# Merge projections of two branches: pairs of tiles by seven block products in place of eight

## The chip, the cores and the metric

The kernel runs on one core of a Trainium2 chip. The metric is the time of one execution on the device in microseconds (us). In the profile the engines are PE (TensorE, matrix products; PEld is its loading of weights), DVE (VectorE), ACT (ScalarE), POOL (GpSimd) and SP (SyncE, which issues most DMAs). Plain loads and stores are issued from SP; DMAs that add to what their destination holds (accumulating DMAs) are issued from POOL.

## What is computed

One layer of a hybrid backbone for 128 context tokens and 512 latent tokens, 640 in all, of width 1024. A gated long convolution (branch h) and an attention (branch a) each give 1024 channels per token. The step that the change touches is the merge of the two:

```python
def merge_branches(y_h, g_h, y_a, g_a, m, w_bh, w_ba, w_out):
    p_h = (y_h * jax.nn.silu(g_h)) @ w_bh
    p_a = (y_a * jax.nn.silu(g_a)) @ w_ba
    m_h, m_a = jnp.split(jax.nn.sigmoid(m), 2, axis=-1)
    return (m_h * p_h + m_a * p_a) @ w_out
```

A residual and a layer norm follow. Everything is float32. The gates m come from the layer's input h by one large projection, which also gives queries, keys, values and the convolution's inputs.

## The kernel before, in words

Activations lie transposed: channels on the 128 partitions, the 640 tokens along the row. A projection tile gives 128 output channels: 8 blocks of 128 input channels (k), for each three passes, and for each pass two matmuls over 320 tokens each, so 48 matmuls of 128x128 weights by 128x320 data. The three passes replace one float32 product: `split` (L96 to L99) writes a high part on ACT (float32r) and the remainder on DVE, and `accumulate` (L160 to L169) adds high x high, low x high and high x low in PSUM. `wtile` (L130 to L148) loads the weights of a tile (512 KB) into the buffer raw (two of them) and splits them into wh (two) and wl (three). With `eng="dma"` the remainder is made otherwise: ACT writes the negative of the raw weights, rounded to float32r, into wl (L142), an accumulating DMA from POOL adds the weights from DRAM to that, which leaves the remainder (L143), and ACT writes wh (L144).

In order of time the kernel does: a prologue; four quarters of the convolution branch, whose results stay in SBUF as eight tiles yh; the attention by pairs of heads, whose results stay as eight tiles ya; woven with it the gate tiles `mix_h` (tanh of half the gate's projection). Then comes the part that is changed. Two tiles of `mix_a` are computed, yh is split, and for n from 0 to 7 the projection T_BH + n is computed from yh and multiplied by (1 + tanh) on DVE (L993), while ya is split. Then, for each n, the next `mix_a` tile, the projection T_BA + n from ya, its gating (L1023), the sum of both branches (L1024) and the split of the sum. `gate_rows` (eight rows of the modulation weights, 16 small matmuls for each two) and `gate_bias` run beside this. Last, five output tiles (L1065) with their norms (L1081 to L1104).

The code is recorded with a tile framework. Its scheduler sets the order of each engine's instructions, by its own forecast of durations, when the kernel is built; on the chip each engine then runs its list strictly in that order, and so do the DMA queues of SP and POOL. During prologue and attention PE's order is that of the code. A buffer of a pool is written again only when its last reader is done, and a DMA that waits for that holds up those behind it on its queue.

Of the kernel before, what the change touches and what calls it, by code (L numbers as in the profile page):

```python
# [15 lines left out]
D = 1024  # L16
LP = 128
LS = 512
NK = 8
# [26 lines left out]
def tile_hyena_natten_step(ctx: ExitStack, tc: tile.TileContext, a, o):  # L46
# [57 lines left out]

    out = {"yh": {}}

    def load_pack(i):
# [10 lines left out]

    hH = hp.tile([P, NK, NT], F32R, tag="hH", name="hH")
    hL = hp.tile([P, NK, NT], F32R, tag="hL", name="hL")  # L120
    st = const.tile([P, NK, 32], F32, tag="st", name="st")
# [48 lines left out]

    def proj(i, xh=None, xl=None, eng=None):
        if i in banks:
            return banks.pop(i)
        w = wtile(i, eng)
        ps = bank(i)
        for k in range(NK):
            accumulate(ps, w, k, xh[k] if xh else hH[:, k], xl[k] if xl else hL[:, k])
            if k < NK - 1:
                yield
        return ps  # L180
# [60 lines left out]
    def prologue():  # L241
# [7 lines left out]
        def work(items, ps):  # L249
            for item in items.split():  # L250
                if item[0] == "w":
                    for _ in range(int(item[1:])):
                        nc.tensor.matmul(ps[:, 256:], hid[:, :P], hid[:, :256], start=True, stop=True, skip_group_check=True)  # L253
                else:
                    i, j = int(item[0]), int(item[1])
                    accumulate(banks[i], early[i], j, hH[:, j], hL[:, j], lead=(0, 1, 2) if j < 1 else (0, 2, 1))

# [18 lines left out]
        for k in range(NK):  # L276
# [32 lines left out]
            for c, s0, n in ((0, PC, LP), (1, SC, LS)):  # L309
                cs = slice(s0, s0 + n)  # L310
                nc.vector.tensor_scalar(hx[:, cs], xt[:, cs], mod[:, 1, c : c + 1], mod[:, 0, c : c + 1], op0=ALU.mult, op1=ALU.add)
                nc.scalar.activation(hH[:, k, cs], xt[:, cs], AF.Identity, scale=mod[:, 1, c : c + 1], bias=mod[:, 0, c : c + 1])  # L312
            nc.vector.tensor_tensor(hL[:, k], hx[:], f(hH[:, k]), op=ALU.subtract)  # L313
            if k == 0:
# [336 lines left out]
    yh, ident = out["yh"], out["ident"]  # L651

# [53 lines left out]
    def values(m):  # L706
# [5 lines left out]
        def passes(k):  # L712
            wh, wl = w[k // 4][0][k % 4], w[k // 4][1][k % 4]
            return ((hH, wh, k == 0, False), (hL, wh, False, False), (hH, wl, False, k == NK - 1))

        for half in range(2):
            ks = range(4 * half, 4 * half + 4)
            for k in ks:
                for x, wk, first, last in passes(k):
                    for t in range(4):  # L720
                        nc.tensor.matmul(  # L721
                            ps[:, t // 2, t % 2 * 256 : t % 2 * 256 + 256], x[:, k, P * t : P * t + P], wk,
                            start=first and t % 2 == 0, stop=last, skip_group_check=True,
                        )
                yield
            if half:
                nc.scalar.activation(v[:, :1024], ps[:].rearrange("p a b -> p (a b)"), AF.Copy)
            else:
                pe = ps_mm.tile([P, 2, 512], F32, tag="mm", name=f"ve{m}")[:, 0]
            for k in ks:  # L730
                for x, wk, first, last in passes(k):
                    nc.tensor.matmul(pe[:, :256], x[:, k, P * 4 :], wk, start=first, stop=last, skip_group_check=True)  # L732
            yield
# [14 lines left out]

    tail = ctx.enter_context(ExitStack())
    ac = ctx.enter_context(ExitStack())  # L750
    ya, tms, edges, biases = [], [], {}, {}

    def attention_setup():
        nonlocal at, mask
        hy.close()
        yap = out["yap"] = tail.enter_context(tc.tile_pool(name="yap", bufs=1, side="right"))
        ya.extend(row(yap, "ya", f"ya{j}", bufs=NK) for j in range(NK))
        at = ac.enter_context(tc.tile_pool(name="at", bufs=1, side="right"))
# [107 lines left out]

    def gated(j, cols, o_):
        nc.vector.tensor_tensor(ya[j][:, cols], out[f"sg{j}"][:, cols], o_, op=ALU.mult)

# [17 lines left out]
    def tiled(i):  # L887
# [39 lines left out]
    def gate_a(j):  # L927
        out[f"sg{j}"] = sg = at.tile([P, NT], F32, tag="sg", bufs=2, name=f"sg{j}") if j else row(yhp, "yh", "sg0")
        yield from gate_tile(T_GA + j, sg[:])
        yield  # L930

    def mix_h():
        homes = ((0, "q"), (0, "k"), (0, "v"), (), (0, "ql"), (0, "kl"), (1, "q"), (1, "ql"))
        for n in range(NK):
            th = slot(*homes[n], f"mh{n}") if homes[n] else th
            th, pair = (pair[:, NT:], None) if n == 3 else (th[:, :NT], th)
# [24 lines left out]

    mp = tail.enter_context(tc.tile_pool(name="mp", bufs=1, side="right"))
    lp = left.enter_context(tc.tile_pool(name="lp", bufs=1))
    gpart = slot(1, "v", "gpart")[:, :D]
    yhH = [row(lp, "yhH", f"yhH{n}", F32R, NK) for n in range(NK)]
    yhL = []
    yaH = [row(mp, "yaH", f"yaH{n}", F32R, NK) for n in range(NK)]
    yaL = []

# [9 lines left out]
    def mix_a(n):  # L979
        ps = now(proj(T_MA + n))[2]  # L980
        th = mp.tile([P, NT], F32, tag="th", bufs=3, name=f"mta{n}")
        nc.scalar.activation(two(th[:]), ps[:, :, :HALF], AF.Tanh, scale=0.5)
        return th

    side = gate_rows()
    mtas = [mix_a(0), mix_a(1)]
    for n in range(NK):
        yhL.append(row(yhp, "yh", f"yhL{n}", F32R))
        split(yhH[n][:], yhL[n][:], yh[n][:])
    for n in range(NK):  # L990
        th = out[f"mh{n}"]
        ps = now(proj(T_BH + n, yhH, yhL))[2]
        nc.vector.scalar_tensor_tensor(two(th), two(th), 1.0, ps[:, :, :HALF], op0=ALU.add, op1=ALU.mult)  # L993
        yaL.append(row(out["yap"], "ya", f"yaL{n}", F32R, NK)[:] if n else slot(1, "kl", "yaL0", F32R)[:, :NT])
        split(yaH[n][:], yaL[n], ya[n][:])
        next(side, None)
    mH, mL = yhH, yhL
    gbc = lp.tile([P, 2, D], F32, tag="gbc", name="gbc")
    eps = lp.tile([P, 1], F32, tag="eps", name="eps")
    nc.gpsimd.memset(eps[:], LN_EPS)  # L1000

    def gate_bias():
        selr = lp.tile([P, 2], F32R, tag="selr", name="selr")
# [3 lines left out]
        gt = out["slots_r"].tile([P, 2, 384], F32R, tag="k", name="gt")  # L1007
        for c0, n in ((0, 384), (384, 384), (768, 256)):
# [8 lines left out]

    for n in range(NK):
# [4 lines left out]
        nc.vector.scalar_tensor_tensor(two(th[:]), two(th[:]), 1.0, ps[:, :, :HALF], op0=ALU.add, op1=ALU.mult)  # L1023
        nc.vector.tensor_tensor(th[:], th[:], out[f"mh{n}"], op=ALU.add)  # L1024
        split(mH[n][:], mL[n][:], th[:])
        next(side, None)
        if n == 4:
            gate_bias()

    wo = []  # L1030
    woh = lp.tile([P, D], F32R, tag="woh", name="woh")
    wol = wp.tile([P, D], F32R, tag="wl", bufs=3, name="wol0")
    wohH = hp.tile([P, 5, D], F32R, tag="hH", name="wohH")
    wolH = hp.tile([P, 5, D], F32R, tag="hL", name="wolH")
    for k in range(NK):
        raw = wp.tile([P, D], F32, tag="raw", name=f"wo{k}")
        load_to(raw[:], a["wall"][T_WO + k])
        if k == 0:
            wo.append((woh[:], wol[:]))
        elif k < 6:  # L1040
            wo.append((wohH[:, k - 1], wolH[:, k - 1]))
        else:
            wh = wp.tile([P, D], F32R, tag="wh", name=f"woh{k}")
            wl = wp.tile([P, D], F32R, tag="wl", bufs=3, name=f"wol{k}")
            wo.append((wh[:], wl[:]))
        split(*wo[k], raw[:])


    tail.close()
    fin = ctx.enter_context(tc.tile_pool(name="fin", bufs=1, side="right"))  # L1050
    bc = fin.tile([P, 2, D], F32, tag="bc", name="bc")
    def out_tile(t, split_cols):
# [188 lines left out]
```

## Time and profile before

| | us |
|---|---|
| median of 3 runs | 927.14 (926.0 to 927.77) |
| the profiled execution | 925.7 |
| its span in the profile | 923.9 |

The mean granted clock of TensorE in the span is 0.997 of full speed. Lines such as `L166 PE MATMUL mm<-hH,wh 128*128 128x320 f32 x1120 | 263.3, 313 | 0.9` are groups: line of the kernel, engine, operation, output tile and input tiles, shape, count, then busy time in us and mean ns of one, then the idle time of the engine just before them in us. A row of a table by stage has the stretch in us, its length, the busy time of PE, PEld, DVE, ACT and POOL with the counts, the granted clock, the share of the 16 DMA engines that was busy, and GB/s. A row of the waits names who waited for whom, the total in us, how often, and the longest. A row of the DMA issues ends with the median us from issue to landing; a row of the DMA queues has packets, MB and the share of the 16 engines' span. Rows of the timeline begin with start and length in us.

### The profile page before, as it was taken

The numbers are of one execution on the slowest core, as the hardware profiler recorded it, in microseconds if no ns is written. First come the engines' busy times: TensorE is split into PE (matmuls) and PEld (weight loads), VectorE is DVE, ScalarE is ACT, GpSimd is POOL, SyncE is SP. The second block draws the span as 40 slices with busy tenths as digits, with TensorE's granted clock in tenths as the row PEclk, the third lists the DMA queues.
The fourth block names the chain that finished last, engine by engine and source line by source line (L and its number), as shares of the span: only waits on it lengthen the run. The fifth ranks groups of instructions, "written<-read, shape, count | busy, mean of one in ns | idle before, by whom it ended". The sixth has DMA issues, their size and how long they took to land.

```text
span 923.9 us, 16758 instructions
## 1 busy us (share of the span) xinstructions
PE 910.2 (99%) x6856; PEld 877.4 (95%) x6856; DVE 486.4 (53%) x948; ACT 380.4 (41%) x776; POOL 146.2 (16%) x188
## 2 busy tenths in 40 slices
PE   8999999999999999999999999999999999999996
PEld 7899999999999999999999999999999999999885
DVE  4776775693796676445352533432261223335676
ACT  4485455554545334255454544444261112223200
POOL 0011010110010000474454543331000000000000
PEclk9999999999999999999999999999999999999998
DMA  8966664655465113242222221212123343224631
GB/s 320 380 161 135 128 149 98 137 133 123 100 141 126 50 49 85 86 122 67 71 68 69 67 70 58 72 49 70 48 69 113 120 146 99 72 69 116 205 114 69
DMA packets 36553, 102.13 MB, mean 111 GB/s; under 512 B 4316, under 2 KB 13020, under 8 KB 36477
## 3 DMA queue, kind: packets, MB, share of 16 engines
q1 hardware_dynamic: 32300, 86.35, 28.9%
q0 software_dynamic: 4032, 14.68, 9.8%
q8 instruction: 54, 0.88, 0.4%
q14 instruction: 23, 0.18, 0.1%
q10 hardware_dynamic: 144, 0.03, 0.0%
HBM read 97.38 MB, written 3.67 MB: 109 GB/s over the span
## 4 chain that ended last, share of the span: by engine, by line
PE 95%; DVE 2%; ACT 2%; issue 1%; POOL 0%; POOLq 0%
PE mm L166 65%; PE out L1065 6%; PE v L721 5%; PE s L788 2%; PE s L831 2%; PE pt L824 2%; PE ve L732 1%; PE adaT L236 1%; PE adaT L253 1%; PE yb L151 1%; PE yb L153 1%; PE yb L152 1%; PE gate L236 0%; PE fl L384 0%; PE fl L385 0%
## 5 line engine op out<-in xcount | busy, mean ns | idle before, releaser
L166 PE MATMUL mm<-hH,wh 128*128 128x320 f32 x1120 | 263.3, 313 | 0.9 <-ACT hH L312 0.6
L166 PE MATMUL mm<-hH,wl 128*128 128x320 f32 x1120 | 259.7, 310 | 0.4 <-DVE wl L99 0.4
L166 PE MATMUL mm<-hL,wh 128*128 128x320 f32 x1120 | 259.1, 310 | 0.0
L99 DVE TENSOR_TENSOR wl<-raw,wh 128x1024 fp32r<-128x1024 f32 x66 | 81.6, 1237 | 231.9 <-ACT wh L98 231.7
L166 PEld LDWEIGHTS mm<-hH,wh 128*128 128x128 f32 x1120 | 186.7, 188 | 6.2 <-issue 4.2
L166 PEld LDWEIGHTS mm<-hH,wl 128*128 128x128 f32 x1120 | 188.0, 188 | 1.4 <-DVE wl L99 1.1
L166 PEld LDWEIGHTS mm<-hL,wh 128*128 128x128 f32 x1120 | 188.2, 188 | 1.1 <-DVE hL L313 0.5
L98 ACT ACTIVATE wh<-raw 128x1024 fp32r<-128x1024 f32 x66 | 69.8, 1059 | 216.8 <-PE mm L166 95.9
L143 POOL DMA_DIRECT2D wl<-wall x28 | 24.3, 869 | 264.0 <-ACT wl L142 208.8
L144 ACT ACTIVATE wh<-raw 128x1024 fp32r<-128x1024 f32 x28 | 29.7, 1060 | 42.9 <-PE mm L166 42.7
L808 POOL TENSOR_SCALAR p<-p,sm 128x384 f32<-128x384 f32 x32 | 42.1, 1326 | 27.7 <-DVE sm L807 27.7
L1095 POOL TENSOR_TENSOR r<-r,bc 128x64 f32<-128x64 f32 x1 | 0.3, 320 | 249.7 <-ACT r L1094 249.7
L808 POOL TENSOR_SCALAR edge<-edge,sm 128x320 f32<-128x320 f32 x32 | 35.5, 1121 | 0.0
L474 DVE SCALAR_TENSOR_TENSOR x<-zs,pack,x 128x641 f32<-128x641 f32 x32 | 28.3, 884 | 12.1 <-ACT x L472 12.0
L826 ACT ACTIVATE pts<-pt 128x384 f32<-128x384 f32 x64 | 26.2, 502 | 11.0 <-PE pt L824 11.0
L142 ACT ACTIVATE wl<-raw 128x1024 fp32r<-128x1024 f32 x28 | 30.0, 1071 | 0.0
L166 PE MATMUL mm<-yhH,wh 128*128 128x320 f32 x128 | 29.9, 315 | 0.0
L166 PE MATMUL mm<-yaH,wh 128*128 128x320 f32 x128 | 29.2, 309 | 0.0
L166 PE MATMUL mm<-yhL,wh 128*128 128x320 f32 x128 | 29.2, 309 | 0.0
L166 PE MATMUL mm<-yaH,wl 128*128 128x320 f32 x128 | 29.2, 309 | 0.0
L166 PE MATMUL mm<-yaL,wh 128*128 128x320 f32 x128 | 29.2, 309 | 0.0
L166 PE MATMUL mm<-yhH,wl 128*128 128x320 f32 x128 | 29.2, 309 | 0.0
(330 smaller groups left out, 1677.7 us busy)
## 6 DMA issues: line engine op xcount, KB each, us to landing
raw<-wall SPq DMA_DIRECT2D x96, 512.0 KB, 3.6
wl<-wall POOLq DMA_DIRECT2D x28, 512.0 KB, 5.8
ada<-wada SPq DMA_DIRECT2D x16, 512.0 KB, 8.1
gate<-wada SPq DMA_DIRECT2D x8, 512.0 KB, 3.7
wo<-wall SPq DMA_DIRECT2D x8, 512.0 KB, 3.7
xt<-xT SPq DMA_DIRECT2D x8, 320.0 KB, 8.1
dec<-decay SPq DMA_DIRECT2D x20, 128.0 KB, 3.5
x<-xB SPq DMA_DIRECT2D x5, 512.0 KB, 3.8
```

The source lines that it names most:

```text
L98: hi = nc.scalar.activation(dst_h, src, AF.Copy)
L99: return hi, (eng or nc.vector).tensor_tensor(dst_l, src, f(dst_h), op=ALU.subtract)
L142: nc.scalar.activation(wl, raw[:], AF.Copy, scale=-1.0)
L143: nc.gpsimd.dma_start(wl, a["wall"][i], accum_op=ALU.add)
L144: nc.scalar.activation(wh, raw[:], AF.Copy)
L166: nc.tensor.matmul(ps[hf][:, :HALF], wt[k], x[:, hf * HALF : (hf + 1) * HALF], start=(i == 0 and k == 0), stop=(i == lead[2] and k == NK - ...
L474: nc.vector.scalar_tensor_tensor(d, zs[:, c : c + NG], convw[:, i, c : c + 1], d, op0=ALU.mult, op1=ALU.add)
L721: nc.tensor.matmul(ps[:, t // 2, t % 2 * 256 : t % 2 * 256 + 256], x[:, k, P * t : P * t + P], wk, start=first and t % 2 == 0, stop=last, ...
L788: nc.tensor.matmul(dst[h], x[rows(h), qs], y[rows(h), ks], start=i == 0, stop=i == 2, skip_group_check=True)
L808: nc.gpsimd.tensor_scalar_mul(pv, pv, sm[:, 2:3])
L826: nc.scalar.activation(ptS[:], pt[:, :384], AF.Copy)
L1065: ins = nc.tensor.matmul(dst, m[k][:, c0 : c0 + P], w[:, c : c + n], start=(first and k == 0), stop=(last and k == NK - 1), skip_group_che ...
```

## The change

The 16 projection tiles of the merge are computed in pairs. For a pair, the 256 output channels and 1024 input channels form a 2x2 block matrix (blocks of 512 input by 128 output channels), and the branch's rows a 2x2 block matrix too (512 channels by 320 tokens). Their product is formed with seven block products by Winograd's form of Strassen's method. Each product is 4 k-blocks x 3 passes = 12 matmuls of 128x320. Sums and differences of blocks come from these places:

- `token_blocks`: yh and ya are written to DRAM when they are ready (16 stores from SP), read back as blocks of 4 x 320 per partition, combined by three subtractions on DVE and one accumulating DMA, and each of the seven is split, once per branch.
- `weight_blocks`: for each pair seven half-tiles of 256 KB are loaded. Two are negated on ACT, four sums (s3, s2, s1, s4) are made by accumulating DMAs; five of the seven are split on ACT and DVE, two (a12, a22) by ACT and an accumulating DMA. Each raw tile has one buffer. The split parts take turns in the five buffers wh (two) and wl (three).
- `pair_product`: the seven products go into four PSUM banks named x, y, v and z, in the order x, y, v, z, x, v, z; between them steps on ACT and DVE form the four results and multiply by the gates.

All eight `mix_a` tiles now come first, ahead of the products. The hL and hH tiles are held as halves, and their memory is used again for token blocks and output weights. Output weights are split during the last pair; `gate_bias` comes after the products.

```diff
     def gate_conv(n):
         if n in half_done:
             gapped_product(out["yh"][n], out[f"u{n // 2}"][n % 2])
+            nc.sync.dma_start(yh_d[n], out["yh"][n][:])
...
             prompt_values(j, spare.pop(0))
+            nc.sync.dma_start(ya_d[j], ya[j][:])
...
+    def token_blocks(src, name):
+        def raw(i, j):
+            t = mg.tile([P, 4, HALF], F32, tag="braw", bufs=4, name=f"{name}{i}{j}")
+            load_to(t[:], src[4 * i : 4 * i + 4, :, HALF * j : HALF * j + HALF].rearrange("k p t -> p k t"))
+            return t[:].rearrange("p k t -> p (k t)")
...
+        t1, t3, t2, t4 = raw(0, 0), raw(0, 1), raw(1, 1), raw(1, 0)
+        yield done(t1, 0)
+        nc.vector.tensor_tensor(t1, t3, t1, op=ALU.subtract)
+        nc.vector.tensor_tensor(t3, t2, t3, op=ALU.subtract)
+        nc.vector.tensor_tensor(t2, t1, t2, op=ALU.subtract)
+        yield done(t2, 1)
+        yield done(t3, 2)
+        yield done(t1, 3)
+        yield done(t4, 4)
+        nc.gpsimd.dma_start(t4, t2, accum_op=ALU.add)
+        yield done(t4, 5)
+        yield done(raw(1, 1), 6)
...
+    def weight_blocks(i0, i1):
+        w0, w1 = ([a["wall"][i][:, 512 * h : 512 * h + 512] for h in range(2)] for i in (i0, i1))
...
+        def halves(r, src=None):
+            n, n_weights[0] = n_weights[0] % 5, n_weights[0] + 1
+            tag = ("wh", "wl", "wh", "wl", "wl")[n]
+            t = wp.tile([P, 2, 512], F32R, tag=tag, bufs=3 if tag == "wl" else 2, name=f"wb{i0}_{n}")
+            if src is None:
+                split(t[:, 0], t[:, 1], r)
+            else:
+                nc.scalar.activation(t[:, 1], r, AF.Copy, scale=-1.0)
+                add(t[:, 1], src)
+                nc.scalar.activation(t[:, 0], r, AF.Copy)
+            return t
+
+        a11 = raw("a11", w0[0])
+        s3, s2 = raw("s3", w1[0]), raw("s2", w1[1])
+        for t in (s3, s2):
+            nc.scalar.activation(t, t, AF.Copy, scale=-1.0)
+        add(s3, w0[0])
+        add(s2, s3)
+        yield halves(a11)
+        yield halves(s2)
+        yield halves(s3)
+        s1 = raw("s1", w1[0])
+        add(s1, w1[1])
+        yield halves(s1)
+        yield halves(raw("a12", w0[1]), w0[1])
+        yield halves(raw("a22", w1[1]), w1[1])
+        s4 = raw("s4", w0[1])
+        add(s4, s2)
+        yield halves(s4)
...
+        for n, t in enumerate("xyvzxvz"):
...
+            w = next(weights)
+            xh, xl = xb(n)
+            for k in range(4):
+                wh, wl = (w[:, i, P * k : P * k + P] for i in range(2))
+                for i, (wk, x) in enumerate(((wh, xh), (wh, xl), (wl, xh))):
+                    nc.tensor.matmul(
+                        dst[t], wk, x[:, k], start=n < 4 and k == 0 and i == 0, stop=k == 3 and i == 2, skip_group_check=True,
+                    )
+            next(step)
+            yield
...
+    for m in range(4):
+        for n, _ in enumerate(pair_product(T_BH + 2 * m, T_BH + 2 * m + 1, out[f"mh{2 * m}"], out[f"mh{2 * m + 1}"], from_yh)):
...
+    for m in range(4):
+        for n, _ in enumerate(pair_product(T_BA + 2 * m, T_BA + 2 * m + 1, mtas[2 * m], mtas[2 * m + 1], from_ya)):
...
-    for n in range(NK):
-        th = mtas.pop(0)
-        if n + 2 < NK:
-            mtas.append(mix_a(n + 2))
-        ps = now(proj(T_BA + n, yaH, yaL))[2]
```

Here `add(dst, src)` is an accumulating DMA from POOL, `raw` a load from SP, and `mg` the pool of the raw tiles.

In the order that the scheduler gives the changed program, PE takes the first product of a pair ahead of the last two of the pair before, and for most pairs then v, y, x (the fifth product), z. The pairs are numbered 0 to 7 below.

More of the change, by code (lines that the diff above doesn't have):

```diff
@@ L650, in tile_hyena_natten_step @@
               8 * NK, N_CONV + N_BACK + N_FILTER)
[L651 removed]
+    ident = out["ident"]
     def rows(h):
@@ L731, in values @@
                 for x, wk, first, last in passes(k):
-                    nc.tensor.matmul(pe[:, :256], x[:, k, P * 4 :], wk, start=first, stop=last, skip_group_check=True)
+                    nc.tensor.matmul(pe[:, :256], x[:, P * 4 :], wk, start=first, stop=last, skip_group_check=True)
             yield
@@ L980, in mix_a @@
         ps = now(proj(T_MA + n))[2]
-        th = mp.tile([P, NT], F32, tag="th", bufs=3, name=f"mta{n}")
+        th = row(yhp, "yh", f"mta{n}")
         nc.scalar.activation(two(th[:]), ps[:, :, :HALF], AF.Tanh, scale=0.5)
-        return th
-    side = gate_rows()
-    mtas = [mix_a(0), mix_a(1)]
-    for n in range(NK):
[L988 to L996, printed above, removed]
@@ L997, in tile_hyena_natten_step, with block, done @@
-    mH, mL = yhH, yhL
-    gbc = lp.tile([P, 2, D], F32, tag="gbc", name="gbc")
-    eps = lp.tile([P, 1], F32, tag="eps", name="eps")
+        return th[:]
+    n_blocks = [0]
+    def block(name):
+        n, n_blocks[0] = n_blocks[0] % 8, n_blocks[0] + 1
+        pool, tag = (blkp, "blk") if n < 4 else (hp, H_TAGS[n - 4])
+        return pool.tile([P, 2, 4 * HALF], F32R, tag=tag, name=name)
+    def token_blocks(src, name):
[3 more added lines that the diff above has]
+            return t[:].rearrange("p k t -> p (k t)")
+        def done(r, n):
+            b = block(f"{name}b{n}")
+            split(b[:, 0], b[:, 1], r)
+            return [b[:, i].rearrange("p (k t) -> p k t", k=4) for i in range(2)]
+        t1, t3, t2, t4 = raw(0, 0), raw(0, 1), raw(1, 1), raw(1, 0)
[10 more added lines that the diff above has]
+        yield done(raw(1, 1), 6)
@@ new lines, in tile_hyena_natten_step, with out_weight @@
+    mH, mL, wo = [], [], []
+    def out_weight(k):
+        raw = wp.tile([P, D], F32, tag="raw", name=f"wo{k}")
+        load_to(raw[:], a["wall"][T_WO + k])
+        t = block(f"wo{k}")
+        wo.append((t[:, 0, :D], t[:, 1, :D]))
+        split(*wo[k], raw[:])
+    for _ in side:
+        pass
+    for m in range(4):
+        for n, _ in enumerate(pair_product(T_BA + 2 * m, T_BA + 2 * m + 1, mtas[2 * m], mtas[2 * m + 1], from_ya)):
+            if m == 3:
+                if n == 0:
+                    out_weight(0)
+                out_weight(n + 1)
+        ns = (2 * m, 2 * m + 1)
+        for n in ns:
+            nc.vector.tensor_tensor(mtas[n], mtas[n], out[f"mh{n}"], op=ALU.add)
+        for n in ns:
+            mH.append(row(yhp, "yh", f"mH{n}", F32R)[:])
+            mL.append(merge_home(n, "mL", F32R))
+            split(mH[n], mL[n], mtas[n])
@@ L1016, in gate_bias @@
                 nc.vector.scalar_tensor_tensor(gbc[:, c, cs], b0[:, cs], 0.25, pg[:, :n], op0=ALU.mult, op1=ALU.add)
-    for n in range(NK):
-        th = mtas.pop(0)
-        if n + 2 < NK:
-            mtas.append(mix_a(n + 2))
-        ps = now(proj(T_BA + n, yaH, yaL))[2]
[L1023 to L1051, printed above, removed]
+    gate_bias()
     def out_tile(t, split_cols):
```

119 lines of the change are left out of this document (95 added, 24 removed).

## Prediction

> **What bounds the kernel now.** I read the page first: busy time, slices, DMA queues, chain of waits.
>
> ```profile
> span 923.9 us, 16758 instructions
> ...
> PE 910.2 (99%) x6856; PEld 877.4 (95%) x6856; DVE 486.4 (53%) x948; ACT 380.4 (41%) x776; POOL 146.2 (16%) x188
> ...
> PEclk9999999999999999999999999999999999999998
> DMA  8966664655465113242222221212123343224631
> GB/s 320 380 161 135 128 149 98 137 133 123 100 141 126 50 49 85 86 122 67 71 68 69 67 70 58 72 49 70 48 69 113 120 146 99 72 69 116 205 114 69
> ...
> q1 hardware_dynamic: 32300, 86.35, 28.9%
> q0 software_dynamic: 4032, 14.68, 9.8%
> ...
> PE 95%; DVE 2%; ACT 2%; issue 1%; POOL 0%; POOLq 0%
> ```
>
> PE is busy for 910.2 of 923.9 us and carries 95% of the chain: every other engine has slack and the DMA engines are one to four tenths busy in the second half. Then the waits of PE, and its busy time in the stretch that the change rebuilds.
>
> ```profile
> PE adaT L253 <- POOL spare L268: 1.5, 1, 1.5
> PE fp L152 <- DVE sl L99: 1.1, 1, 1.1
> ```
>
> ```profile
> 696.70:850.00 153.30, 153.30 (x1133) 150.17 (x1132) 50.80 (x57) 34.38 (x40) 0.00 (x0) 1.00 0.32 103
> ```
>
> The longest wait of PE in the whole run is 1.5 us, and from 696.7 to 850 us it does not idle at all (153.30 of 153.30). So a matmul taken out here shortens the run by its full time, and every wait put in lengthens it by its full time; there is no slack on PE to absorb one.
>
> **What is taken from PE.** The two branch projections are six groups of 128 matmuls (first and last by the groups by line), and the timeline gives their spacing.
>
> ```profile
> L166 PE MATMUL mm<-yhH,wh 128*128 128x320 f32 x128 | 29.9, 315 | 0.0
> ...
> L166 PE MATMUL mm<-yhH,wl 128*128 128x320 f32 x128 | 29.2, 309 | 0.0
> ```
>
> ```profile
> 696.72 0.46 PE L166 MATMUL mm<-yhH,wh 128*128 128x320 f32 x2
> ...
> 703.47 0.46 PE L166 MATMUL mm<-yhH,wl 128*128 128x320 f32 x2
> ```
>
> One tile is 24 such rows of two. From the first start to the last are 23 steps: 6.75 / 23 = 0.2935 us, or 0.1467 us per matmul (the 309 ns are its latency; they overlap). Before: 6 x 128 = 768, or 112.7 us. The changed program holds 8 pairs x 7 products x 12 = 672, or 98.6 us. **PE gains 14.1 us.** In the old order two neighbours share their weights and in the new one none do; the value projection shows that case.
>
> ```profile
> 335.95 0.64 PE L721 MATMUL v<-wh,hH 128*128 128x256 f32 x4
> 336.43 0.29 PE L721 MATMUL v<-wh,hL 128*128 128x256 f32 x1
> ```
>
> Four matmuls with four different weights take 0.48 us, 0.120 each for 256 columns, against 0.147 for 320: the same rate per column. Other weights each time cost nothing. Without any new wait the profiled execution's 925.7 us (span 923.9 and 1.8 around it) would become 911.6.
>
> **What is added for DMA.** A pair loads seven 256 KB half-tiles and adds six more by accumulating DMAs on POOL. One product lasts 12 x 0.1467 = 1.76 us, a pair 12.3 us. The issues by line and the groups give the prices.
>
> ```profile
> raw<-wall SPq DMA_DIRECT2D x96, 512.0 KB, 3.6
> wl<-wall POOLq DMA_DIRECT2D x28, 512.0 KB, 5.8
> ...
> tb<-rpbT SPq DMA_DIRECT2D x16, 128.0 KB, 2.1
> ```
>
> ```profile
> L98 ACT ACTIVATE sh<-sd 128x512 fp32r<-128x512 f32 x20 | 12.8, 638 | 17.6 <-DVE sd L390 11.7 <-PE yb L152 5.9
> ```
>
> A 256 KB load lies between 2.1 and 3.6: I take 2.7. A 256 KB accumulate is not in this trace: above by 5.8 (twice the size), below by 2.7 (a plain load). I take 4.5, 5.8 less about what half the size saves a plain load, since it is the same operation. A negation on ACT is 0.64. Three things then stand against PE:
>
> *The reused slot.* Five slots hold the split half-tiles, so the fifth product's (weights a12) is written only when the last product of the pair before has been read. In the built order of PE just two products stand between, plus two matmuls: 2 x 1.76 + 0.29 = 3.8 us. Negation and accumulate take 0.64 + 4.5 = 5.1. PE waits 1.3 us in each of some six pairs.
>
> *The chain of sums.* s3 is loaded, negated, accumulated; s2 accumulates s3; only then is s3's single buffer loaded again: 2.7 + 0.64 + 4.5 + 4.5 and handoffs is 12.5 to 13 us against the 12.3 of a pair. PE overtakes it slowly.
>
> *The order on POOL.* Its queue is in order. In pair 1, s2's accumulate stands behind that of a22 of the same pair, which waits for the first product to free its slot; behind s2's stand s4's and, on PE, the second product. In pair 3 the accumulate of a12 stands behind s3's and s2's of pair 4: issued about 8 us later than its slot allows. On SP the last two gate rows wait for buffers that PE frees only by running earlier gate matmuls, and PE waits for them before pair 1's second product.
>
> I walked the four queues from the end of the last mix_a tile (T0) with these prices, each DMA as if alone. Waits of PE: pairs 0 and 1 together 4.7 us, pair 2 2.1, pair 3 8.7, pairs 4 and 5 1.4 and 1.8, pair 6 3.4, pair 7 1.9; **24 us**.
>
> They are not alone. By the queue rows above, plain traffic costs 28.9% of 923.9 / 86.35 = 3.1 us of all 16 engines per MB, accumulating 9.8% of 923.9 / 14.68 = 6.2. At its best (second slice, 380 GB/s at nine tenths) plain is 2.4, so accumulating, at the same ratio, 4.8. After T0 come some 21.7 MB plain (seven pairs 12.8, gate rows 3.1, blocks of the attention branch 2.6, output weights 3.1) and 12.8 MB accumulating: 114 us at best, 146 at the mean rates. PE wants 98.6 + 5 for the gate rows, 103.6. So the DMA engines alone hold PE up by 10 to 42 us. Between the walk's 24 (prices of idle engines) and 42 I take **31 us**; the ends are 0 (accumulates as quick as plain loads, rates at best, pair 0's prepared weights lasting) and 50 (the walk's waits on top of slower DMAs).
>
> The Trainium skill, "DMA: Bandwidth & Descriptors", section "Anatomy of one DMA — SWDGE (gpsimd) path", fits a POOL DMA as about 2.0 us plus bytes over 436 GB/s. For 512 KB that is 3.2 us; the trace has 5.8 for its accumulates, so it does not agree for these, and for 256 KB it would say 2.6, which is the first rival's case below.
>
> **What lies beside other work.** DVE gains 14 block splits and 6 differences of 1280 columns and loses the 16 splits of 640; ACT likewise.
>
> ```profile
> L99 DVE TENSOR_TENSOR sl<-sd,sh 128x512 fp32r<-128x512 f32 x20 | 13.8, 688 | 4.1 <-PE mm L166 3.1 <-ACT sh L98 0.9
> ...
> L560 DVE TENSOR_TENSOR W<-X,F 128x1280 f32<-128x1280 f32 x4 | 6.0, 1489 | 0.0
> ```
>
> 20 x 1.49 + 40 weight splits x 0.69 + about 56 gate steps x 0.5 = 86 us over 160 us, where DVE had 51 in 153: it stays under PE, and I cost it at nothing. If that cover went, a late split would cost its 0.7 per product. All mix_a tiles first: the same 56 us of PE in one piece, in which yh's blocks and pair 0's weights are made; its weights' loads stand on SP behind twelve new loads (4.5 MB, 14 us at 3.1) but two tiles (14 us) are loaded ahead: 0, at most 2. The 16 stores of branch rows stand on SP between weight loads.
>
> ```profile
> SPq L63 <- DVE wl L99: 304.9, 56, 13.9
> ```
>
> SP mostly waits for buffers that DVE frees, so a store whose row is done costs an issue; one placed too early holds up the next load. I take 1 us, 0 to 4. At the end gate_bias and the last output weights come after the merge pool is freed, and the first two output tiles finish together; DVE sat idle between tiles,
>
> ```profile
> 893.24 1.28 DVE L1081 TENSOR_TENSOR r<-gbc,out 128x512 f32<-128x512 f32 x2 [4.04 <-PE out L1065]
> ```
>
> 4 us each, which takes up the lump: 1 us, 0 to 5.
>
> **The sum.** 925.7 - 14.1 + 31 + 1 + 1 = 944.6. The median of the runs shown, 927.1, is 1.4 above the profiled execution: **946**.
>
> **Rivals.**
> *Accumulates are quick.* If 256 KB accumulates land in some 2.7 us, a12 is ready after 3.3 of its 3.8 us, the chain of sums takes 9 of 12.3, POOL's order does no harm, and the DMA engines run near their best rate. PE waits 0 to 10: 913 to 925, faster. For it: the lead of pair 0 and DMA engines that stood at 0.32. Against it: the 5.8 us median of 28 issues, most of them on engines that were not full. It decides at about 3.2 us per accumulate.
> *DMA and clock.* Waits of 3 us and more could lower the granted clock.
>
> ```profile
> 914.80:924.00 9.20, 0.80 (x7) 0.60 (x6) 4.64 (x11) 0.74 (x2) 0.93 (x2) 0.68 0.16 57
> ```
>
> In the 9.2 us after the last product, where PE is idle, the clock is 0.68. At that rate for two products (3.5 us) after each of eight waits: 8 x 3.5 x (1/0.68 - 1) = 13 us, so 959; with the DMA engines at the mean rate (42) 970. The Trainium skill, "TensorE: Matmul & The Clock Gate", "Part 1: The HAM clock gate (the "warmup" mystery)", halves the clock after an idle window of about 3.4 us; the trace's last stretch agrees in sign, and no wait before it is long enough to show it.
> *It balances*: waits of 12 to 16, 925 to 929.
> That the change does not do what it says is out: 672 matmuls stand in the built program.
>
> **Chances.** Forecast (about 932 to 957) 0.50, DMA and clock 0.21, quick accumulates 0.23, balance 0.06. A measurement of this kernel tells about 0.2% (1.9 us) from no change. Faster 0.23, same 0.06, slower 0.71. The range, 917 to 968, leaves out about 0.08 of the quick end and 0.07 of the slow; the likeliest case's own is 932 to 957.
>
> **What would show it.** Right: PE with 96 matmuls fewer, and in the list of waits of PE the accumulating DMA or the splits behind it, 20 us and more in total, from about 739 us on; DMA share above 0.7 there; the accumulates landing in 4 to 6 us. Wrong: PE busy without gaps through the products (then 913), landings under 3.2 us, or PE waiting instead for mix_a's weights, for the blocks of yh, or in the output tiles.

## The result, and the profile after

The changed kernel takes 991.75 us (median of 4 runs, 989.44 to 994.14), the kernel before 926.57 beside it: a ratio of 1.0705, 95% interval 1.0674 to 1.0735. The prediction said 946, at most 968: the sign was right, the size short by 46 us.

The page of the changed kernel, with the lines that answer to those of before:

```profile
span 992.4 us, 17028 instructions
...
PE 919.9 (93%) x6760; PEld 879.1 (89%) x6760; DVE 529.6 (53%) x1032; ACT 423.5 (43%) x854; POOL 189.4 (19%) x238
...
PE   8999999999999999999999999999996667667995
...
PEclk9999999999999999999999999999998778898998
...
q1 hardware_dynamic: 45644, 104.44, 32.1%
q0 software_dynamic: 11232, 28.58, 17.4%
```

PE has the 96 matmuls fewer (6856 to 6760), but in slices 31 to 37 it is six or seven tenths busy, and the clock falls in most of the same slices. Next the busy time by stretch (PE, PEld, DVE, ACT, POOL, then granted clock, DMA share, GB/s): the stage of the gate tiles, and then two of the nine rows of the products.

```profile
680.00:740.00 60.00, 60.00 (x411) 60.00 (x410) 21.68 (x19) 21.79 (x27) 5.08 (x6) 1.00 0.55 169
```

```profile
760.00:780.00 20.00, 12.67 (x114) 10.71 (x114) 6.75 (x12) 4.89 (x9) 4.35 (x5) 0.74 1.01 269
...
840.00:860.00 20.00, 11.44 (x57) 10.45 (x58) 9.10 (x13) 7.63 (x12) 4.66 (x6) 0.83 0.87 206
...
sum 180.00, PE 123.08 PEld 112.47 DVE 85.39 ACT 69.81 POOL 38.69; mean PE 13.68 PEld 12.50 DVE 9.49 ACT 7.76 POOL 4.30
```

Up to the first product nothing is lost: 60.00 of 60.00. Of the 180 us from 740 to 920 PE is busy in 123. The waits of PE (in total, times, longest):

```profile
PE sp L1111 <- DVE tu L1080: 14.6, 8, 7.5
PE sp L1111 <- DMA wb<-wall: 13.3, 5, 3.5
PE gate L246 <- DMA gate<-wada: 11.1, 4, 4.5
PE sp L1111 <- ACT tu L1083: 6.4, 2, 4.6
PE sp L1111 <- DVE tc L1080: 4.1, 5, 1.1
PE sp L1111 <- ACT wb L1051: 3.4, 5, 0.7
```

With three smaller rows these are 57 us. `tu` and `tc` are tiles that the steps of `pair_product` write on DVE (`tu` on ACT too). The prediction had counted the busy time of these steps and put nothing for PE waiting on them. A row names only the releaser that came last, so a long wait for `tu` can have a late split behind it. And the DMAs land late (KB each, us from issue to landing):

```profile
s<-wall SPq DMA_DIRECT2D x32, 256.0 KB, 5.0
a<-wall SPq DMA_DIRECT2D x24, 256.0 KB, 6.6
s<-wall POOLq DMA_DIRECT2D x16, 256.0 KB, 6.0
s<-s POOLq DMA_DIRECT2D x16, 256.0 KB, 4.4
...
wb<-wall POOLq DMA_DIRECT2D x16, 256.0 KB, 7.0
```

The walk had taken 2.7 for a load and 4.5 for an accumulate. The trace of before has four loads of this size in its early stages, where the DMA engines were six to nine tenths busy:

```profile
w<-fw SPq DMA_DIRECT2D x4, 256.0 KB, 6.7
```

### The profile page after: what moved, and what is told of

The parts are those of the page before. It is cut to its first block, busy times and chain, and to the rows that moved or that the text cites. A ratio compares the mean times of both kernels' runs of the same rounds, so it can differ in the third digit from the quotient of the medians.

```text
span 992.4 us, 17028 instructions
## 1 busy us (share of the span) xinstructions
PE 919.9 (93%) x6760; PEld 879.1 (89%) x6760; DVE 529.6 (53%) x1032; ACT 423.5 (43%) x854; POOL 189.4 (19%) x238
## 5 line engine op out<-in xcount | busy, mean ns | idle before, releaser
L99 DVE TENSOR_TENSOR wl<-raw,wh 128x1024 fp32r<-128x1024 f32 x50 | 62.7, 1257 | 196.5 <-ACT wh L98 196.3
L98 ACT ACTIVATE wh<-raw 128x1024 fp32r<-128x1024 f32 x50 | 52.9, 1060 | 138.4 <-PE mm L176 70.5
L1111 PE MATMUL sp<-yhb,wb 128*128 128x320 f32 x336 | 63.1, 350 | 22.2 <-DVE tu L1080 9.4
L1111 PE MATMUL sp<-yab,wb 128*128 128x320 f32 x336 | 60.3, 337 | 23.6 <-DMA wb<-wall 6.8
L1111 PEld LDWEIGHTS sp<-yhb,wb 128*128 128x128 f32 x336 | 58.5, 220 | 26.7 <-DVE tu L1080 9.9
L1111 PEld LDWEIGHTS sp<-yab,wb 128*128 128x128 f32 x336 | 55.8, 210 | 28.0 <-DMA wb<-wall 7.6
L154 ACT ACTIVATE wh<-raw 128x1024 fp32r<-128x1024 f32 x28 | 29.6, 1059 | 42.9 <-PE mm L176 42.7
L1212 PE MATMUL out<-wo,mH 128*128 128x512 f32 (+1 forms) x176 | 45.8, 376 | 0.0
L98 ACT ACTIVATE wb<-s 128x512 fp32r<-128x512 f32 x32 | 19.9, 624 | 52.2 <-PE sp L1111 38.8
L1212 PEld LDWEIGHTS out<-wo,mH 128*128 128x128 f32 x176 | 31.7, 188 | 6.7 <-DVE tc L1080 0.2
L1042 POOL DMA_DIRECT2D s<-wall x16 | 15.3, 976 | 115.8 <-DMA a<-wall 46.0
```

Source lines behind the costliest of these rows:

```text
L98: hi = nc.scalar.activation(dst_h, src, AF.Copy)
L99: return hi, (eng or nc.vector).tensor_tensor(dst_l, src, f(dst_h), op=ALU.subtract)
L154: nc.scalar.activation(wh, raw[:], AF.Copy)
L1042: nc.gpsimd.dma_start(dst, src, accum_op=ALU.add)
L1111: nc.tensor.matmul(dst[t], wk, x[:, k], start=n < 4 and k == 0 and i == 0, stop=k == 3 and i == 2, skip_group_check=True,)
L1212: ins = nc.tensor.matmul(dst, m[k][:, c0 : c0 + P], w[:, c : c + n], start=(first and k == 0), stop=(last and k == NK - 1), skip_group_che ...
```

## The experiments

Three questions: what the accumulating DMAs cost, and by what; why PE waits for DVE; and what lowers the clock. A fourth set then tries to keep the gain. Kernels with an interval were timed in several rounds, the others run once beside the kernel before. The four runs of the changed kernel lie between 989.44 and 994.14, so a difference of 2 or 3 us from a single run says nothing.

### The accumulating DMAs

**Two halves split instead of accumulated.**

```diff
-        yield halves(raw("a12", w0[1]), w0[1])
-        yield halves(raw("a22", w1[1]), w1[1])
+        yield halves(raw("a12", w0[1]))
+        yield halves(raw("a22", w1[1]))
```

> Only the two half-tiles a12 and a22 are split on ACT and DVE in place of ACT and an accumulating DMA; the four sums still go through DMAs. Theory of the reused slot (a12 must be written and landed in 3.8 us): PE's waits for DMA wb (13.3 us) and ACT L1051 (3.4) vanish, DMA has a third less to accumulate: 955 to 972. Theory of the chain s3, s2, s4 alone: the waits move to the sums and the time stays at 980 to 992.

Measured: 972.5. Two of six accumulates gone, 19 us gone: half a microsecond above the range of the theory of the reused slot, and well below the other's. The waits for DMA `wb` and ACT L1051 are gone, as that theory said. But the waits for `tc` (11.1) and `tu` (8.2 on DVE, 9.1 on ACT) are 28.4 us now, against 25.1 in the changed kernel.

**Two buffers for the chain of sums.**

```diff
-            t = mg.tile([P, 512], F32, tag=tag, name=f"{tag}_{i0}")
+            t = mg.tile([P, 512], F32, tag=tag, bufs=2 if tag in ("s2", "s3") else 1, name=f"{tag}_{i0}")
```

> The raw tiles s2 and s3 get two buffers each in place of one, nothing else. Theory of the chain (a sum can start only when the pair before has let go of its buffer): the loads of the next pair come early and 20 us or more go: under 972. Theory of full DMA engines: the same bytes have to pass, 985 to 995.

Measured: 972.1, at the edge of what the theory of the chain expected. So the chain of sums was a part, also of 20 us. No run makes both edits, so whether the two parts add up or overlap is not shown.

**A quarter of the bytes.**

```diff
-            nc.gpsimd.dma_start(dst, src, accum_op=ALU.add)
+            nc.gpsimd.dma_start(dst[:, :128], src[:, :128], accum_op=ALU.add)
```

> Every accumulating DMA of weights adds only 128 of its 512 columns (the other columns lack their sum), so the count of DMAs, their order and all waits stay, and their bytes fall to a quarter. Theory of full DMA engines: their work after 739 us falls by some 9 MB of accumulation, 60 us of engine time, and the landings to under 4 us: 935 to 955. Theory of count and order (queues wait whatever the size): 970 to 990.

Measured: 954.0. The same count of accumulates and the same order on POOL, 38 us less: most of their price goes with their bytes.

**None at all.**

```diff
         def add(dst, src):
-            nc.gpsimd.dma_start(dst, src, accum_op=ALU.add)
+            pass
```

> The changed kernel with every accumulating DMA of the weight sums left out (the loads, negations and splits stay, so the sums and two remainders are wrong; the blocks of the branch outputs keep theirs). Theory of the loaded accumulates: with a quarter of the columns added the time had come to 954; with none the rest of what they cost goes: 925 to 942, waits of PE after 739 us of 10 to 20 us, clock at 0.99 or more. Rival, the five slots and the in-order queues of ACT and DVE: these stay as they are, so the time stays near the 946 of the kernel with sums on GpSimd, 943 to 955, with 25 us of waits.

Measured: 939.3, 52.4 below the changed kernel: the weight accumulates and all that follows from them. The waits of PE after 739 us are still over 20 us, of which 15.2 for `tc` and `tu` (19 waits, none over 2.0). That is what neither theory had explained.

**The sums on GpSimd.**

```diff
-            nc.gpsimd.dma_start(dst, src, accum_op=ALU.add)
...
+            nc.gpsimd.tensor_tensor(t[:], p, q, op=op)
...
+        (a11, a12), (a21, a22) = raw("w0", i0), raw("w1", i1)
+        s3 = combine("s3", a11, a21, ALU.subtract)
+        s2 = combine("s2", s3, a22, ALU.subtract)
```

> The seven block products stay; no weight goes through an accumulating DMA. A pair loads its two whole tiles (512 KB each), GpSimd's own adder forms the four sums, and all seven half-tiles are split on ACT and DVE. Theory (the half-tiles come late because of the accumulating DMAs and their chain): the waits of PE in the products fall from 57 us to under 10, the granted clock goes back to 1.0, and the time is 912 to 922, under the kernel before (926.6). Rival (five slots and the in-order lists of ACT and DVE hold PE whatever makes the sums): 950 or more.

Measured: 946.5, ratio 1.0215 (1.0198 to 1.0232), between the two expectations. Waits for `tc` and `tu` are 17.1 us here too.

### Why PE waits for DVE

One pair in the kernel without accumulates, by the timeline (start, us, engine, line, operation, and in brackets the idle time before it and its releaser):

```profile
839.22 0.49 DVE L1080 TENSOR_TENSOR tc<-sp,tu 128x320 f32<-128x320 f32 x1 [0.40 <-PE sp L1111]
...
839.85 2.00 PE L1111 MATMUL sp<-yab,wb 128*128 128x320 f32 x12 [0.68 <-DVE tc L1080]
...
841.89 0.49 DVE L1080 TENSOR_TENSOR tc<-sp,tu 128x320 f32<-128x320 f32 x1 [0.80 <-PE sp L1111]
...
842.53 3.77 PE L1111 MATMUL sp<-yab,wb 128*128 128x320 f32 x24 [0.68 <-DVE tc L1080]
...
846.33 0.49 DVE L1080 TENSOR_TENSOR tu<-sp,tu 128x320 f32<-128x320 f32 x1 [0.33 <-PE sp L1111]
...
846.88 7.30 PE L1111 MATMUL sp<-yab,wb 128*128 128x320 f32 x48 [0.58 <-DVE tu L1080]
```

One product, two products, four products: three breaks in this pair, and most pairs have them at the same places. Each time DVE reads v, z or y and PE may go on only when it has. From 839.85 to 842.53 are 2.68 us for a product of 1.76, so a break costs 0.92 with the drained pipeline; the other two cost 0.83 and 0.94 (the four products ahead of the first row began at 831.87). That is some 2.7 us in a pair. Eight full pairs would make 21, more than the 14.1 that the missing products save; there were 19 such waits and not 24.

What ties them is one line: `both = ps_mm.tile([P, 2, 512], ...)` holds x beside y, and another v beside z. The banks differ, but the tile is one, and the built program lets PE write z only after DVE has read v. At the pair's end the next v also takes the tile that z has just left. The edit gives each of the four a tile and a bank of its own:

```diff
-            if n in (0, 2):
-                both = ps_mm.tile([P, 2, 512], F32, tag="mm", name=f"sp{i0}_{n}")
-                dst.update(zip("xy" if n == 0 else "vz", (both[:, 0, :HALF], both[:, 1, :HALF])))
+            if n < 4:
+                dst[t] = aux(f"sp{t}{i0}")[:, :HALF]
```

In the changed kernel:

> The changed kernel with the four outputs x, y, v, z of a pair in a PSUM bank and tile each (before: two tiles of two banks, x with y and v with z); the gate rows take the place in the other pool. DMAs, sums and slots as they are. Theory of the shared tiles: in the kernel without weight accumulates PE waited three times in each pair for the DVE step that had just read the neighbour in the same tile, 0.58 to 0.68 us and 0.2 of drained pipeline each; these go, so the waits for DVE tu and tc (18.7 us in the changed kernel) fall by 10 or more, and what hangs on the accumulating DMAs stays: 970 to 985. Rival, all is DMA: these waits only stood in for late splits, PE then waits for the DMAs instead: 988 to 996.

Measured: 972.1, 19.7 less; in the built order of PE y stands ahead of v again, so tile and order changed together. What PE waits for now:

```profile
PE spy L1110 <- ACT wb L98: 12.4, 3, 5.9
PE spv L1110 <- DMA wb<-wall: 11.7, 2, 7.7
PE gate L246 <- DMA gate<-wada: 9.1, 2, 5.4
PE spv L1110 <- DVE tu L1080: 3.7, 1, 3.7
PE spx L1110 <- DMA wb<-wall: 3.1, 3, 1.7
PE spx L1110 <- ACT wb L98: 1.6, 1, 1.6
```

Few and long: DMAs, and splits of sums that DMAs make. In the kernel without accumulates:

> The kernel without weight accumulates (sums and remainders wrong as there), with the four outputs in own banks. Theory of the shared tiles: 24 waits of some 0.65 us with their 0.2 of drain go, 15 to 20 us: 917 to 926, waits of PE after 739 us at most 7 us. Rival, slots and queues: the same waits come back as waits for splits: 933 to 941.

Measured: 919.0, 20.3 less. The recurring breaks are gone; the one wait of PE over 1.5 us in the whole run is

```profile
PE spx L1110 <- ACT tu L1083: 3.2, 1, 3.2
```

The two causes add up: 52.4 and 19.7 alone, 72.8 together (991.75 to 918.95). With the sums on GpSimd:

> The kernel with the sums on GpSimd (946.5) and the four outputs in own banks. Theory of the shared tiles: 13 to 20 us less, 926 to 934. Rival, DVE splits stretched beside GpSimd and five slots hold PE anyway: 938 to 947.

Measured: 930.9, 15.6 less; ratio to before 1.0044 (1.0027 to 1.0061). That is 11.9 us above the kernel without accumulates, and no run takes it apart. One thing in it is DVE beside GpSimd. Splits of the changed kernel, and of the kernel with the sums on GpSimd (first version), in the groups from 740 to 900 us:

```profile
L99 DVE TENSOR_TENSOR wb<-s,wb 128x512 fp32r<-128x512 f32 x26 | 17.7, 686 | 10.0 <-ACT wb L98 10.0
```

```profile
L99 DVE TENSOR_TENSOR wb<-s,wb 128x512 fp32r<-128x512 f32 x30 | 26.6, 894 | 7.3 <-ACT wb L98 7.3
```

686 ns become 894 when GpSimd adds in SBUF, while DVE's steps `tu` and `tc`, which read PSUM, stay at 0.48 to 0.49 us.

**Seven slots, sums in place.** More slots for split halves; the room comes from the tiles of the sums, which are now written over halves already split.

```diff
-            n, n_weights[0] = n_weights[0] % 5, n_weights[0] + 1
-            tag = ("wh", "wl", "wh", "wl", "wl")[n]
+            n, n_weights[0] = n_weights[0] % 7, n_weights[0] + 1
+            tag = ("wh", "wl", "wh", "wl", "wl", "wx", "wx")[n]
...
+        combine(a11, a11, a21, ALU.subtract)
```

> As the last, with the sums written over halves that are already split, and two more slots for split halves in the room that this frees (seven, one for each product). If the slots then hold the splits back: 5 to 12 us below the last run, 915 to 924, which would beat the kernel before. If not: within 3 us of the last run.

Measured: 954.2, ratio 1.0296 (1.0272 to 1.0320): a miss, 23 us the wrong way. PE's waits after 739 us grow from 12.2 to 26.6 us, 9.3 of them in the output tiles. In its timeline the load of a pair waits until the halves of the pair before have been summed and split, and load, sums and splits stand in a row at each pair's start. Slots and places of the sums changed together, so this run does not say which did the harm; the last run of this section has the slots alone.

### The clock

**Fillers.** Six matmuls that nobody reads, after each product of the changed kernel.

```diff
+            fill = aux(f"fill{i0}_{n}")
+            for _ in range(6):
+                tc.keep_in_program_order(nc.tensor.matmul(fill[:, :HALF], xh[:, 0, :P], xh[:, 0], start=True, stop=True, skip_group_check=True))
```

> The changed kernel with six matmuls of 320 columns that nobody reads after each of the 56 products (49 us of PE in all, at 0.1467 each), on operands that are ready. They fill part of each wait of PE and change no DMA. If it is the waits that lower the clock: granted clock 0.97 or more in the rows from 740 to 920, a product alone in 1.8 to 1.9 us, and 985 to 1010 us in all (49 more, 25 to 30 less of waits, 12 to 19 less of clock). If it is the traffic of the DMA engines: clock of 0.74 to 0.91 as before in the rows where the DMA share is near 1, and 1015 or more.

Measured: 1006.9. The time is where waits as the cause put it, 49 us of added matmuls for 15 us of time; but the clock rows are 0.83 to 1.00 and not 0.97, since waits up to 6.7 us were left. Alone it settles nothing, so the next run makes waits without the traffic.

**Long waits alone.** In the kernel without accumulates and with own banks, PE waits once in each pair for two small DMAs.

```diff
+            if n == 0:
+                d = mg.tile([P, 4], F32, tag="dwait", bufs=2, name=f"d{i0}")
+                nc.scalar.activation(d[:, :2], dst["x"][:, :2], AF.Copy)
+                nc.gpsimd.dma_start(wait_d[:], d[:, :2])
+                nc.gpsimd.dma_start(d[:, 2:], wait_d[:])
+            if n == 1:
...
+                tc.keep_in_program_order(nc.tensor.matmul(pw[:, 0, :2], f(xh[:, 0, :P]), d[:, 2:], start=True, stop=True, skip_group_check=True))
```

> The kernel with own banks and no accumulates (919.0, sums wrong as there), in which PE waits once in each pair, ahead of the third product, for two DMAs of 1 KB each, one behind the other, that start from the first product's result: eight waits of 4 to 6 us with little traffic added. If waits of PE lower the clock: rows from 740 to 880 at 0.75 to 0.9, products at 2.0 us and more behind a wait, 919 + 36 to 48 of waits + 8 to 20 of clock: 963 to 985. If the accumulating traffic lowered it: clock at 0.98 or more, 955 to 967.

Measured: 987.7, span 985.9, 68.7 more than without the waits. Its waits, one stretch, and PE's timeline behind one of them:

```profile
PE pw L1123 <- DMA d<-wait_d: 48.4, 8, 8.7
```

```profile
780.00:800.00 20.00, 16.25 (x86) 16.02 (x86) 6.52 (x12) 6.26 (x12) 1.08 (x2) 0.76 0.39 81
```

```profile
779.71 0.56 PE L1123 MATMUL pw<-d,yhb 128*128 128x2 f32 x2 [7.50 <-DMA d<-wait_d]
780.13 3.55 PE L1111 MATMUL spv<-yhb,wb 128*128 128x320 f32 x12
783.48 2.68 PE L1111 MATMUL spz<-yhb,wb 128*128 128x320 f32 x12
786.00 1.92 PE L1111 MATMUL spx<-yhb,wb 128*128 128x320 f32 x12
787.76 1.92 PE L1111 MATMUL spv<-yhb,wb 128*128 128x320 f32 x12
...
796.95 0.56 PE L1123 MATMUL pw<-d,yhb 128*128 128x2 f32 x2 [3.75 <-DMA d<-wait_d]
797.37 3.55 PE L1111 MATMUL spv<-yhb,wb 128*128 128x320 f32 x12
```

The waits are longer than planned (48.4 us in place of 36 to 48, so the time is 3 us above the range), and the clock is 0.76 with the DMA engines at 0.39. From start to start the first product takes 3.35 us in place of 1.76, the second 2.52, the third 1.76: after a long wait PE runs at half speed for some five microseconds, which costs 1.59 + 0.76 = 2.35 us. The stretch behind the wait has the clock at 0.50 while the DMA engines stand still (0.00):

```profile
780.20:785.00 4.80, 4.80 (x19) 4.80 (x19) 1.11 (x2) 0.63 (x1) 0.00 (x0) 0.50 0.00 2
```

Eight such are 19; 48.4 + 19 = 67 of the 68.7. So waits alone do lower the clock. The last two lines of the timeline show it after 3.75 us too. The kernel without accumulates (shared tiles) had waits up to 2.0 us and full DMA engines, and its clock stayed at 1.00:

```profile
740.00:760.00 20.00, 16.28 (x179) 14.16 (x178) 15.34 (x19) 10.90 (x18) 0.00 (x0) 1.00 1.02 334
```

The Trainium skill, "TensorE: Matmul & The Clock Gate", "Part 1: The HAM clock gate (the "warmup" mystery)", gives half the clock after an idle window of about 3.4 us; these rows agree.

For shorter waits the length of one wait does not decide it in these runs. Here are two products behind a wait of 3.16 us (own banks, no accumulates), behind one of 2.59 us (the version with early sums and own banks, below), and behind waits of 1.21 and 1.46 us with only 0.6 us of matmuls between them (sums on GpSimd, first version):

```profile
807.57 3.95 PE L1110 MATMUL spx<-yab,wb 128*128 128x320 f32 x24 [3.16 <-ACT tu L1083]
```

```profile
806.23 5.33 PE L1108 MATMUL spx<-yab,wb 128*128 128x320 f32 x24 [2.59 <-ACT tu L1081]
```

```profile
763.53 6.46 PE L1099 MATMUL sp<-yhb,wb 128*128 128x320 f32 x24 [1.46 <-DVE tc L1068]
```

At full speed two products take some 3.8 us by this measure. The longest of these waits left the clock at 1.00 (800 to 820 us); in the other two runs the rows fell to 0.91 and 0.83. When a short wait costs the clock is left open.

### The sums made before the products

The sums depend on weights alone, and the DMA engines had slack in the attention stage. First with the same negations and accumulating DMAs, moved there, and the results kept in DRAM:

```diff
+    def early_sums():
...
+            for t in (s3, s2):
+                nc.scalar.activation(t, t, AF.Copy, scale=-1.0)
+            yield
+            nc.gpsimd.dma_start(s3, w0[0], accum_op=ALU.add)
+            nc.gpsimd.dma_start(s1, w1[1], accum_op=ALU.add)
...
+        for src in (w0[0], s2, s3, s1, w0[1], w1[1], s4):
+            yield halves(src)
```

> The four sums of all eight pairs are made in the attention stage with the same negations and accumulating DMAs and stored in DRAM (48 accumulates less 16 that a12 and a22 needed, 8 MB of stores); the product stage loads seven plain halves of 256 KB per pair and splits all of them on ACT and DVE with the same five slots. Theory of the loaded accumulates: 915 to 930, since loads land in 3 to 4 us and nothing hangs on a chain. Rival, five slots and queues: 935 to 945, waits of PE of 20 us and more as in the kernel with sums on GpSimd, but with DVE at 0.69 a split. A cost of the move would show as a wait of PE of more than 5 us in total between 300 and 700 us.

Measured: 982.4, ratio 1.0636 (1.0581 to 1.0690), far above both expectations. The product stage came out as in the kernel without accumulates (778.25 to 922.16, 144 us, against 738.67 to 879.72, 141), shared tiles and all. But it began 40 us late. The groups of ACT from 380 to 620 us show why:

```profile
L937 ACT ACTIVATE es<-es 128x512 f32<-128x512 f32 x16 | 10.1, 632 | 62.0 <-DMA es<-wall 55.0 <-issue 7.1
```

ACT runs in order; its negations stood ahead of the attention's work and waited 55 us for their loads, and PE then waited 27.0 us for ACT (`ptsp` 20.7, `v` 6.3). Most of the rest is the clock: PE's busy time is 914.5 us against 901.9 without accumulates, 12.6 more for the same matmuls, and the clock is 0.91 from 400 to 500 us. What the accumulates themselves cost there was not parted from it.

> As the run with the sums made early, with seven slots for split halves in place of five, one for each product of a pair. If the slots hold the splits back: 5 to 15 us below that run, 908 to 920, waits of PE under 10 us. If they do not: within 2 us of it.

Measured: 986.1, ratio 1.0652 (1.0621 to 1.0682): no gain. It is 3.7 us above five slots, and the runs of the two kernels overlap (983.7 to 989.7, and 980.9 to 991.2).

Then with what the runs had taught: nothing on ACT, four GpSimd instructions in place, loads and stores held at their places in SP's order, own banks.

```diff
+            for dst, p, q, op in ((a11, a11, a21, ALU.subtract), (a21, a21, a22, ALU.add), (a22, a11, a22, ALU.subtract), (a12, a12, a22, ALU.add)):
+                nc.gpsimd.tensor_tensor(dst, p, q, op=op)
+            yield
+            for i in range(2):
+                pinned_load(sums_d[m][i][:], w[i][:])
```

> The four sums of a pair are made in the attention stage by four GpSimd instructions in place, one pair for each pair of heads, and stored in DRAM; the product stage loads seven plain halves per pair, has the four outputs in own banks and five slots. No weight accumulates anywhere, and nothing left out. If shared tiles and accumulates are the whole of the loss: products and tail as in the kernel with own banks and no accumulates (178.6 us from the end of the last mix_a tile), the attention stage at most 6 us longer: 917 to 926, at or below the kernel before. Rival, the sums disturb the attention stage as the early accumulates did (38 us later at the first product): 930 to 960. Rival, seven splits on DVE per pair are too many without the four negations and two remainders on ACT and DMA: waits for wb of 8 us and more, 926 to 935.

Measured: 919.9, ratio 0.9936 (0.9923 to 0.9949): 0.6% below the kernel before. The page, its first stretch of products, and the longest wait of PE:

```profile
span 916.7 us, 17032 instructions
...
PE 899.3 (98%) x6760; PEld 864.7 (94%) x6760; DVE 537.8 (59%) x1048; ACT 405.5 (44%) x822; POOL 192.9 (21%) x222
```

```profile
740.00:760.00 20.00, 20.00 (x174) 17.85 (x176) 17.70 (x24) 8.59 (x14) 0.00 (x0) 1.00 0.96 315
```

```profile
PE spx L1108 <- ACT tu L1081: 2.6, 1, 2.6
```

In this stretch PE has no gap with the DMA engines at 0.96, and the clock is at 1.00: plain loads may fill the engines if nothing hangs on their order.

> As e13 with seven slots for split halves. If slots hold splits back: 2 to 6 us below e13. If not, within 1.5 us of it.

Measured: 918.8, ratio 0.9923 (0.9907 to 0.9939), the best version, but by 1.1 us, less than what was set as no difference: slots do not hold PE in this kernel.

## Why the prediction was wrong in size

- **PE gains 14.1**: held in kind, 96 matmuls fewer and no wait ahead of the first product, and nearly in size. Counted from the start of each matmul to the start of the next, waits left out, the branch projections took 114.1 us before, and the products take 101.5 in the kernel with own banks and no accumulates: 12.6. The best version stands 7 us below the kernel before and not 14.
- **Stores on SP, all gate tiles first (1 us, 0)**: held. Not a wait from 680 to 740 us, and the first product starts at 738.59.
- **DVE's steps beside other work, costed at nothing**: failed. DVE had the time (85 of 180 us busy), but the shared tiles put the latency of three steps per pair between PE's products. 20 us, shown twice by own banks (19.7 and 20.3, with the order of the products changed as well). Busy shares could not show it; the line `both = ps_mm.tile(...)` and PE's order could.
- **Waits for the accumulates, 31 us**: the mechanism was right, the term too small. With own banks, the six rows of waits shown above are 41.6 us against 3.2 without accumulates, so 38 us of waits. Most of the rest of the 53 us goes with the clock: PE's busy time is 912.5 us against 899.8, 12.7 more for the same matmuls. The prices were those of engines with slack: accumulates landed in 4.4 to 7.0 and not 4.5, loads in 5.0 to 6.6 and not 2.7. "A 256 KB load lies between 2.1 and 3.6" did not hold even in the trace of before, which had 6.7 in its busy early stages. The slot (with its two accumulates) and the chain were each shown to be worth some 20 us, but not what both are worth together; the order on POOL was not tried by itself.
- **The clock, kept as a rival with a chance of 0.21**: it was part of any case with waits of 4 to 7 us. Its own estimate was 13 us, from a mean clock of 0.68; behind a long wait it is 0.50. In the changed kernel PE's busy time is 919.9 us against 901.9 without accumulates, 18 us for the same matmuls.
- **Accumulates quick (913 to 925), balance (925 to 929)**: out, whatever the accumulates' price: with none at all, but with the shared tiles, the time is 939.

In sum: 925.7 - 14.1 + 20 (shared tiles) + 53 (accumulates: waits 38, clock some 13, about 2 unassigned) = 984.6, against the median of 991.75. The other 7 us are also in the kernel with own banks and no accumulates (919.0 against 925.7 - 14.1 = 911.6): 3.2 are its one long wait, 1.5 the products (12.6 in place of 14.1), 1.7 the gate rows, which take PE 6.2 us in place of 4.6 and are cut into more pieces; about 1 is left open.

## What to carry to other kernels

Price every wait of an engine that has no slack by the order of its own instructions: what must have been read before the next write, tile by tile as the program tracks it, and not only bank by bank. A chain of DMAs is priced at the load of the stage that it runs in, and any wait of some 4 us and more costs PE another 2 us behind it, and shorter waits close together can cost as much. Work on constants belongs in a stage with slack, on an engine that nothing critical stands behind.

## What the runs showed of the hardware

- After a wait of 3.75 us or more PE ran at half speed: 12 matmuls of 320 columns in 3.35 us, then 2.52, then 1.76. DMA engines at 1.02 of their time did not lower the clock. In the kernel without accumulates waits up to 2.0 us did not either, but with the sums on GpSimd waits of 1.21 and 1.46 us close together did, and so did one of 2.59 us in the version with early sums, where one of 3.16 us without accumulates did not.
- A split of 128x512 on DVE took 894 ns on average in place of 686 when GpSimd added in SBUF beside it; steps with one operand in PSUM kept their 0.48. The Trainium skill, "SBUF — State Buffer", "Who interferes with whom", says that a DVE instruction with two SBUF inputs contends with a GpSimd instruction that reads SBUF; the rows agree.
- Accumulating DMAs of 256 KB at a DMA share of 0.46 to 1.04 landed in 4.4 us from SBUF and 6.0 to 7.0 from DRAM.
